# Planned attention: the inverse norms of queries and keys are spread by ScalarE instead of Pool

## The chip, the cores and the metric

The kernel runs on one core of a Trainium2 chip. The metric is the device time of one execution in microseconds (us); the number quoted for a kernel is the median of its runs. The engines are called as in the profile: PE multiplies matrices (PEld is its weight load, which overlaps), DVE is VectorE, ACT is ScalarE, POOL is GpSimd, SP issues most DMAs.

## What is computed

A causal trunk of two layers over 512 tokens of width 1024, float32 in and out. Layer 0 mixes with attention, layer 1 with a gated short convolution, and each is followed by a gated MLP of width 2816 with a width-3 convolution. Only the attention is touched:

```python
xn = rms_norm(h, norm_g)
proj = xn @ w_in                       # q, k, v of 16 heads of 64, and 8 gate logits
q_fox = rms_norm(q[:, :H_FOX], fox_q_gain)   # per head, over its 64 columns
k_fox = rms_norm(k[:, :H_FOX], fox_k_gain)
q_sb  = rms_norm(q[:, H_FOX:], sb_q_gain)
k_sb  = rms_norm(k[:, H_FOX:], sb_k_gain)
o_fox = forgetting_attention(q_fox, k_fox, v[:, :H_FOX], log_f)   # softmax with a decay
o_sb  = stick_breaking_attention(q_sb, k_sb, v[:, H_FOX:])        # sigmoids and a running product
return concat(o_fox, o_sb) @ w_out
```

`rms_norm` divides by the root of the mean square of the 64 columns of a head. The inverse norms are what the change handles.

## The kernel before, in words

Features lie on the 128 partitions and the 512 tokens along the free dimension. Each product of two float32 matrices is made of three PE passes: every operand is split into a rounded part `hi` (made by ACT) and a rest `lo` (made by DVE), and PE adds hi·hi, lo·hi and hi·lo into one PSUM bank (`mm3`, L435 to L440, for weights as the stationary operand; `mm3_rhs`, L620 to L623, for the values). Weights stream from HBM in tiles of about 0.5 MB (`raw`), which ACT copies to `whi` (L750) and DVE subtracts to `wlo` (L752).

The attention works on pairs of heads, eight pairs, in the order 4, 5, 6, 7 (stick-breaking), 0, 1, 2, 3 (forgetting). For each pair `queries_keys` (L885) does this:

- two dense projections into PSUM, 24 matmuls each, one for queries and one for keys; ACT evicts them (L908 or L916) and squares them (L913, L917);
- PE sums the squares over each head's 64 columns with a matrix of ones (L924), ACT copies the sums to SBUF (L927), and PE turns them so that tokens lie on the partitions (L928);
- DVE makes the inverse roots in a chain of small instructions, each of which needs the one before: L933, L945, three steps of Newton's method (L516 to L537), and L949. Their result is `qr`, 128 tokens by 16 numbers;
- **the spread, L960**: each of these numbers is written 64 times side by side into a tile `y` of 128 by 512, so that the four transposes of PE that follow (L967) put the inverse norm of each token under each of the head's 64 rows;
- DVE multiplies (L971), ACT makes `hi` (L973), DVE makes `lo` (L974). The scores of the pair (L1124) need these.

For the four forgetting pairs both queries and keys take this way; for the four stick-breaking pairs the queries alone, since the keys' norm goes into the scale of the sigmoid. So there are 4·2 + 4·1 = 12 spreads.

The order of the work in this part is not the order of the code. Every step is handed to a planner (`Plan`, L60 to L265) as an operation with an engine, a cost in us, what it reads and writes, and a rank. `order` (L191) lists the operations greedily: at each point it takes the engine that can begin something first, by its table of costs, and on that engine the operation of lowest rank among those that can begin within 0.03 us. A finished operation is seen by others after a fixed delay (`AFTER`: DVE 0.12, ACT 0.15, POOL 0.1). `choose` (L164) does so 60 times with the costs varied by up to 4%, replays each list four times with costs varied by 5%, and keeps the list that ends first on average. Dense projections are fillers: they have the highest ranks and go where nothing more urgent can begin on PE. The chosen list is issued in that order, and each engine then works through its own instructions strictly in order. An operation that the planner moves or re-prices can therefore move any other.

After the planned part (attention and its output projection) the rest of the kernel, MLP, convolution and second MLP, is written in program order and is the same in both kernels.

Of the kernel before, what the change touches and what calls it, by code (L numbers as in the profile page):

```python
# [23 lines left out]
AF = mybir.ActivationFunctionType  # L24
# [3 lines left out]
P = 128  # L28
S = 512
NB = S // P  # L30
# [4 lines left out]
HD = 64  # L35
# [233 lines left out]
def trunk(  # L269
# [7 lines left out]
    act, dve, pe, pool = nc.scalar, nc.vector, nc.tensor, nc.gpsimd  # L277
# [12 lines left out]
    def f32(ap):  # L290
        return ap.bitcast(F32)
# [125 lines left out]
    def weights(ahead=AHEAD):  # L417
        while len(ready) < min(len(wanted), at[0] + 1 + ahead):
            ready.append(load(len(ready)))
            split_all(len(ready) - 1)  # L420
        at[0] += 1
        return ready[at[0] - 1]
# [5 lines left out]
    def halves_of(x):  # L428
        return x.rearrange("p (two c) -> p two c", two=2)

    def sorted_(acc):

        return acc.rearrange("p (c two) -> p two c", two=2)
# [211 lines left out]
    plan = Plan()  # L645
# [48 lines left out]
    def DVE(us, fn, **k):  # L694
        return plan.op("DVE", us, fn, **k)

    def ACT(us, fn, **k):
        return plan.op("ACT", us, fn, **k)

    def PE(us, fn, **k):  # L700
        return plan.op("PE", us, fn, **k)

    def series(steps, r, w, rank, us=0.075):

        for i, fn in enumerate(steps):
            names[0] += 1
            key = ("series", names[0])
            DVE(us, fn, r=r, w=[key] if i < len(steps) - 1 else [key, *w], rank=rank)
            r = [key]
# [69 lines left out]
    def dense_part(bank_, w, k, part, seq):  # L779


        def fn():
            hi, lo = (turns(t) for t in x_of(k))
            w_hi, w_lo = w.get(k)
            if part:
                pe.matmul(bank_.tile, w_hi, lo, start=False, stop=k == ND - 1)
            else:
                pe.matmul(bank_.tile, w_hi, hi, start=k == 0, stop=False)
                pe.matmul(bank_.tile, w_lo, hi, start=False, stop=False)
        o = PE(0.216 if part else 0.432, fn, r=[*w.keys(k), (("hi", "lo")[part], k)], w=[bank_], rank=FILLER + seq)  # L790
        o.chunk = w.number
# [86 lines left out]
    def project_head(i, w, seq, ahead):  # L878
        b = acc_()
        for k in range(ND):  # L880
            dense(b, slice(None), w, k, lambda k=k: x_of(k), [("hi", k), ("lo", k)], k == 0, k == ND - 1, seq,
                  ahead=ahead if k == 0 else ())
        return b

    def queries_keys(p, ws, seq):  # L885

        fox, at0 = p < 4, CORE + 100 * PLACE[p]
        kept, sqs, got = {}, {}, {}
        banks = {}
        if seq is None:  # L890
            b = [acc_() for _ in range(2)]
            for k in range(ND):
                for part in range(2):
                    for i in range(2):
                        dense_part(b[i], ws[i], k, part, -FILLER + 20 + k + (ND * i if k >= 4 else 0))
            banks = dict(enumerate(b))
        for i in range(2):
            fixed = i == 1 and not fox
            if fixed:
                got[i] = half_["hi", i](), half_["lo", i]()  # L900
            else:
                kept[i] = kept_()
            b = banks[i] if i in banks else project_head(i, ws[i], seq + i, got[i] if fixed else [kept[i]])
            g = head_gains[:, (0 if fox else 2) + (1 - i):][:, 0:1]
            sq = sqs[i] = sq_()
            if fixed:
                hi, lo = got[i]
                ACT(0.57, lambda b=b, hi=hi, g=g: act.activation(halves_of(hi.tile), sorted_(b.tile), AF.Copy, scale=g),  # L908
                    r=[b, "head_gains"], w=[hi], rank=EVICT)
                DVE(0.66, lambda b=b, hi=hi, lo=lo, g=g: dve.scalar_tensor_tensor(  # L910
                    halves_of(lo.tile), sorted_(b.tile), g, halves_of(f32(hi.tile)), op0=ALU.mult, op1=ALU.subtract),
                    r=[b, hi, "head_gains"], w=[lo], rank=EVICT)
                ACT(0.49, lambda b=b, sq=sq: act.activation(halves_of(sq.tile), sorted_(b.tile), AF.Square), r=[b], w=[sq], rank=EVICT)  # L913
            else:
                n = kept[i]
                ACT(0.49, lambda b=b, n=n: act.activation(halves_of(n.tile), sorted_(b.tile), AF.Copy), r=[b], w=[n], rank=EVICT)  # L916
                ACT(0.52, lambda n=n, sq=sq: act.activation(sq.tile, n.tile, AF.Square), r=[n], w=[sq], rank=at0)  # L917

        t_sum, mid = turn_(), mid_()

        def sums():
            for i in range(2):
                for b in range(NB):
                    pe.matmul(t_sum.tile[32 * b:32 * (b + 1), 0:P], head_ones[:, i, :], sqs[i].tile[:, b * P:(b + 1) * P],  # L924
                              start=i == 0, stop=i == 1, tile_position=(0, 32 * b))
        PE(0.57, sums, r=[sqs[0], sqs[1]], w=[t_sum], rank=at0 + 2, mode="col", ahead=[mid])
        ACT(0.16, lambda: act.activation(mid.tile, t_sum.tile[:, 0:P], AF.Copy), r=[t_sum], w=[mid], rank=at0 + 2)  # L927
        PE(0.11, lambda: pe.transpose(t_sum.tile[:, P:2 * P], mid.tile, ident), r=[mid], w=[t_sum], rank=at0 + 2)  # L928
        made = {}

        def scaled():
            made["v"] = tiny.tile([P, NB, 4], F32, tag="qv", name=f"qv{p}")
            dve.tensor_tensor(  # L933
                made["v"], t_sum.tile[:, P:2 * P].rearrange("p (b c) -> p b c", b=NB)[:, :, 0:4], rx2[:, :, None].to_broadcast([P, NB, 4]), op=ALU.mult)
        DVE(0.09, scaled, r=[t_sum, "rx2"], w=[("v", p)], rank=at0 + 3)

        def v_():
            return made["v"].rearrange("p b i -> p (b i)")

        def r_():  # L940
            return made["r"].rearrange("p b i h -> p (b i h)")

        def add():
            made["r"] = tiny.tile([P, NB, 2, 2], F32, tag="qr", name=f"qr{p}")
            dve.tensor_scalar(v_(), v_(), EPS, None, op0=ALU.add)  # L945

        def by_norm():
            rf = made["r"].rearrange("p b i h -> p b (i h)")
            dve.tensor_tensor(rf, rf, norm.col[:, :, None].to_broadcast([P, NB, 4]), op=ALU.mult)  # L949
        series([add] + rsqrt(r_, v_, 16, f"qk{p}") + [by_norm], [("v", p)], [("r", p)], at0 + 3)  # L950
        if not fox:
            s = q_scale[p] = scales_()
            DVE(0.075, lambda: dve.tensor_copy(s.tile[:, 0], made["r"][:, :, 1, :]), r=[("r", p)], w=[(s, 0)], rank=at0 + 6)
            DVE(0.075, lambda: dve.tensor_scalar(s.tile[:, 1], made["r"][:, :, 1, :], -1.0, None, op0=ALU.mult),
                r=[("r", p)], w=[(s, 1)], rank=at0 + 6)
        for i in kept:
            t, wide, n = turn_(), y_(), kept[i]

            def spread(wide=wide, i=i):
                pool.tensor_copy(  # L960
                    wide.tile.rearrange("p (b h d) -> p b h d", b=NB, h=2),
                    made["r"][:, :, i, :][:, :, :, None].to_broadcast([P, NB, 2, HD]))
            plan.op("POOL", 1.0, spread, r=[("r", p)], w=[wide], rank=at0 + 4)

            def rows(t=t, wide=wide):
                for b in range(NB):
                    pe.transpose(t.tile[:, b * P:(b + 1) * P], wide.tile[:, b * P:(b + 1) * P], ident)  # L967
            hi, lo = got[i] = half_["hi", i](), half_["lo", i]()
            PE(0.436, rows, r=[wide], w=[t], rank=at0 + 4, ahead=[hi, lo])
            g = head_gains[:, (0 if fox else 2) + (1 - i):][:, 0:1]  # L970
            DVE(0.66, lambda t=t, n=n, g=g: dve.scalar_tensor_tensor(  # L971
                n.tile, n.tile, g, t.tile, op0=ALU.mult, op1=ALU.mult), r=[t, "head_gains"], w=[n], rank=at0 + 5)
            ACT(0.52, lambda n=n, hi=hi: act.activation(hi.tile, n.tile, AF.Copy), r=[n], w=[hi], rank=at0 + 5)  # L973
            DVE(0.6, lambda n=n, hi=hi, lo=lo: dve.tensor_tensor(lo.tile, n.tile, f32(hi.tile), op=ALU.subtract), r=[n, hi], w=[lo], rank=at0 + 5)  # L974
        halves[p] = got
# [384 lines left out]
    with tc.tile_pool(name="mlp0", bufs=1) as mp:  # L1360
# [3 lines left out]
        for o in range(ND):  # L1364
            acc = bank("ab"[o % 2])
            k = 0
            for nk in (8, 7, 7):
                w = weights()
# [7 lines left out]
    with tc.tile_pool(name="mix", bufs=1) as mp:  # L1376
# [23 lines left out]
        for o in range(ND):  # L1400
            w = weights()
# [7 lines left out]
    with tc.tile_pool(name="mlp1", bufs=1) as mp:  # L1409
# [13 lines left out]
        for c in range(2):  # L1423
# [23 lines left out]
            for k in range(k0):  # L1447
                if k % 2 == 0:
                    w = weights()
# [42 lines left out]
```

## Time and profile before

| what | value |
|---|---|
| median of 3 runs | 1116.42 us (1116.28, 1119.06, 1116.42) |
| the profiled execution's own time | 1118.01 us |
| its span, first to last instruction | 1116.2 us |
| granted PE clock | 1.000 |
| busy: PE / PEld / DVE / ACT / POOL | 1109.1 / 960.1 / 715.0 / 477.8 / 26.1 us |
| the 12 spreads on POOL | 10.7 us |

The profile shows one execution. A row of a timeline gives the start in us, the duration, engine, line, instruction, what it writes and reads, and in brackets how long its engine was idle just before and who ended that. Rows of the same kind that follow each other may be merged (x2). The duration of a matmul is a modelled one that overlaps its successor; the distance from start to start is what the matmul costs PE. A row of the windows view gives, for a stretch of time, each engine's busy time and its number of instructions.

### The profile page before, as it was taken

The page shows a single profiled execution, that of the slowest core. Times are in us where ns is not written, and L with a number is a line of the kernel's source. Part 1 is how long each engine was busy: PE and PEld are TensorE (multiplying, and loading weights), DVE is VectorE, ACT ScalarE, POOL GpSimd, SP SyncE. Part 2 cuts the span into 40 slices and gives each one's busy share as a digit, 9 for nine tenths or more (in the row PEclk, how much of TensorE's full clock was granted, in tenths as well). Part 3 has the DMA queues.
Part 4 walks back from the last instruction along what each step waited for, and adds up shares of the span by engine and source line. Part 5 has one row for each costly group of instructions (what it writes and reads, how often), then busy time and mean ns, then how long its engine had stood idle before and what let it go on. Part 6 is the DMA issues. An engine that isn't in the chain of part 4 may idle for free.

```text
span 1116.2 us, 14711 instructions
## 1 busy us (share of the span) xinstructions
PE 1109.1 (99%) x5781; PEld 960.1 (86%) x5781; DVE 715.0 (64%) x1117; ACT 477.8 (43%) x722; POOL 26.1 (2%) x92
## 2 busy tenths in 40 slices
PE   9999999999999999999999999999999999999998
PEld 8888788888888888888888888888888888888887
DVE  5898666767777777753334655556877777772322
ACT  6676655545444444432332323233444444442120
POOL 4000100000000000000000000000000000000000
PEclk9999999999999999999999999999999999999999
DMA  8434221223333333333333333333544333333441
GB/s 207 106 74 114 58 76 39 77 76 95 113 95 102 106 95 110 95 104 98 96 102 113 95 97 111 95 112 105 127 120 123 95 111 97 97 134 110 141 143 38
DMA packets 220933, 114.40 MB, mean 102 GB/s; under 512 B 39900, under 2 KB 213260, under 8 KB 220864
## 3 DMA queue, kind: packets, MB, share of 16 engines
q1 hardware_dynamic: 202416, 109.10, 33.5%
q10 hardware_dynamic: 18064, 4.20, 1.7%
q8 instruction: 45, 0.74, 0.3%
q0 software_dynamic: 384, 0.17, 0.1%
q14 instruction: 24, 0.20, 0.1%
HBM read 109.25 MB, written 4.19 MB: 102 GB/s over the span
## 4 chain that ended last, share of the span: by engine, by line
PE 91%; DVE 5%; DMA 1%; issue 1%; ACT 1%; SPq 1%; POOL 0%; DVEq 0%; POOLq 0%; ACTq 0%
PE psb L438 12%; PE psb L439 12%; PE psb L440 12%; PE psa L438 10%; PE psa L439 10%; PE psa L440 10%; PE acc L438 2%; PE acc L440 2%; PE acc L439 2%; PE psa L621 2%; PE psa L622 2%; PE psa L623 2%; PE psb L621 2%; PE psb L622 2%; PE psb L623 2%; PE score L1195 1%
## 5 line engine op out<-in xcount | busy, mean ns | idle before, releaser
L405 ACT ACTIVATE whi<-raw 128x1024 fp32r<-128x1024 f32 (+1 forms) x163 | 171.1, 1050 | 278.0 <-PE psb L439 97.0
L406 DVE TENSOR_TENSOR wlo<-raw,whi 128x1024 fp32r<-128x1024 f32 (+1 forms) x163 | 197.1, 1209 | 122.3 <-ACT whi L405 121.6
L438 PE MATMUL psb<-hs_hi,whi 128*128 128x512 f32 x480 | 182.7, 381 | 0.0
L439 PE MATMUL psb<-hs_lo,whi 128*128 128x512 f32 x480 | 181.9, 379 | 0.0
L440 PE MATMUL psb<-hs_hi,wlo 128*128 128x512 f32 x480 | 181.9, 379 | 0.0
L438 PE MATMUL psa<-hs_hi,whi 128*128 128x512 f32 x416 | 158.2, 380 | 0.0
L439 PE MATMUL psa<-hs_lo,whi 128*128 128x512 f32 x416 | 157.7, 379 | 0.0
L440 PE MATMUL psa<-hs_hi,wlo 128*128 128x512 f32 x416 | 157.7, 379 | 0.0
L553 DVE SCALAR_TENSOR_TENSOR u<-y,taps,u 128x510 f32<-128x510 f32 (+1 forms) x176 | 131.0, 747 | 5.2 <-ACT u L550 2.4
L440 PEld LDWEIGHTS psb<-hs_hi,wlo 128*128 128x128 f32 x480 | 90.7, 189 | 12.9
L439 PEld LDWEIGHTS psb<-hs_lo,whi 128*128 128x128 f32 x480 | 90.7, 189 | 12.6
L438 PEld LDWEIGHTS psb<-hs_hi,whi 128*128 128x128 f32 x480 | 90.7, 189 | 12.6
L440 PEld LDWEIGHTS psa<-hs_hi,wlo 128*128 128x128 f32 x416 | 78.6, 189 | 11.2
L439 PEld LDWEIGHTS psa<-hs_lo,whi 128*128 128x128 f32 x416 | 78.6, 189 | 11.0
L438 PEld LDWEIGHTS psa<-hs_hi,whi 128*128 128x128 f32 x416 | 78.6, 189 | 11.0
L545 ACT ACTIVATE a<-u 128x512 fp32r<-128x512 f32 x44 | 27.7, 630 | 118.0 <-DVE u L1347 118.0
L550 ACT ACTIVATE u<-y,taps 128x512 f32<-128x512 f32 x88 | 62.6, 714 | 12.0 <-DVE y L1335 12.0
L1335 DVE TENSOR_TENSOR y<-psb,nrow_n 128x512 f32<-128x512 f32 x44 | 30.4, 691 | 57.9 <-PE psb L440 57.9
L1346 ACT ACTIVATE u<-u 128x512 f32<-128x512 f32 x44 | 27.7, 629 | 85.9 <-DVE u L553 85.8
L752 DVE TENSOR_TENSOR wlo<-raw,whi 128x1024 fp32r<-128x1024 f32 (+2 forms) x41 | 43.8, 1075 | 19.0 <-ACT whi L750 18.8
L546 DVE TENSOR_TENSOR a<-u,a 128x512 fp32r<-128x512 f32 x44 | 30.4, 691 | 25.1 <-ACT a L545 25.1
L438 PE MATMUL acc<-hs_hi,whi 128*128 128x512 f32 x112 | 44.6, 398 | 0.0
(263 smaller groups left out, 1948.8 us busy)
## 6 DMA issues: line engine op xcount, KB each, us to landing
raw<-in_ffn_w_up SPq DMA_DIRECT2D x88, 512.0 KB, 3.8
raw<-in_ffn_w_down SPq DMA_DIRECT2D x30, 512.0 KB, 3.6
raw<-in_conv_w_in SPq DMA_DIRECT2D x24, 512.0 KB, 3.7
raw<-in_attn_w_in SPq DMA_DIRECT2D x20, 512.0 KB, 4.0
raw<-in_ffn_w_down SPq DMA_DIRECT2D x16, 448.0 KB, 3.3
raw<-in_attn_w_out SPq DMA_DIRECT2D x8, 512.0 KB, 3.4
raw<-in_conv_w_out SPq DMA_DIRECT2D x8, 512.0 KB, 3.5
big<-in_x SPq DMA_DIRECT2D x8, 256.0 KB, 4.2
```

The lines of the kernel that those rows point to most:

```text
L405: made = act.activation(hi[:, at_], raw[:, at_], AF.Copy)
L406: dve.tensor_tensor(lo[:, at_], raw[:, at_], f32(hi[:, at_]), op=ALU.subtract)
L438: pe.matmul(acc, w[0], hi, start=first, stop=False)
L439: pe.matmul(acc, w[0], lo, start=False, stop=False)
L440: pe.matmul(acc, w[1], hi, start=False, stop=last)
L546: dve.tensor_tensor(lo, src, f32(hi), op=ALU.subtract)
L550: act.activation(dst, src, AF.Copy, scale=tap(2))
L553: dve.scalar_tensor_tensor(dst[:, d:], src[:, 0:S - d], tap(j), dst[:, d:], op0=ALU.mult, op1=ALU.add)
L621: pe.matmul(acc, lhs[0], w[0], start=first, stop=False)
L622: pe.matmul(acc, lhs[0], w[1], start=False, stop=False)
L623: pe.matmul(acc, lhs[1], w[0], start=False, stop=last)
L752: DVE(dve_us(per * n), lambda: dve.tensor_tensor(self.lo.tile[:, at_], self.raw.tile[:, at_], f32(self.hi.tile[:, at_]), op=ALU.subtract), ...
```

## The change

The spread is issued on ACT, as an activation that copies, and no longer on POOL, and the planner is told so, with a cost of 0.49 us and no longer 1.0:

```diff
             def spread(wide=wide, i=i):
-                pool.tensor_copy(
+                act.activation(
                     wide.tile.rearrange("p (b h d) -> p b h d", b=NB, h=2),
-                    made["r"][:, :, i, :][:, :, :, None].to_broadcast([P, NB, 2, HD]))
-            plan.op("POOL", 1.0, spread, r=[("r", p)], w=[wide], rank=at0 + 4)
+                    made["r"][:, :, i, :][:, :, :, None].to_broadcast([P, NB, 2, HD]), AF.Copy)
+            plan.op("ACT", 0.49, spread, r=[("r", p)], w=[wide], rank=at0 + 4)
```

No other operation is added or removed: PE has the same matmuls on both sides, DVE and SP as many instructions as before, ACT has 12 more and POOL 12 fewer. But the planner makes a new list, and the order on every engine changes. Three places show it.

ACT, the first spread of all (pair 4; `y` is the spread tile, `qr` the inverse norms, `sq` squares, `qk_hi` rounded keys or queries, `whi` rounded weights, `v` values). Before:

```order
L917 ACTIVATE sq_511<-u_177_394 128x512
L908 ACTIVATE qk_hi_188_466<-acc_465,head_gains 128x512
L913 ACTIVATE sq_575<-acc_465 128x512
L750 ACTIVATE whi_585<-raw_479 128x1024
L1017 ACTIVATE v_556<-acc_555,ncol_n_445 128x256
L973 ACTIVATE qk_hi_211_634<-u_173_376 128x512
```

With the change:

```order
L917 ACTIVATE sq_502<-u_178_396 128x512
L908 ACTIVATE qk_hi_188_464<-acc_463,head_gains 128x512
L913 ACTIVATE sq_580<-acc_463 128x512
L960 ACTIVATE y_589<-qr_520 128x512
L750 ACTIVATE whi_598<-raw_472 128x1024
L1017 ACTIVATE v_562<-acc_561,ncol_n_436 128x256
L973 ACTIVATE qk_hi_205_601<-u_173_376 128x512
```

The spread stands between two activations that do not need it: the weights' copy and the eviction of values now stand behind an instruction that waits for DVE's chain.

PE, the transposes of pair 2, one of the forgetting pairs (`w` are attention weights that are turned, `acc` the banks of the values' projection). Before:

```order
L622 MATMUL acc_2474<-wlo_2520,hs_hi 128x256
L623 MATMUL acc_2474<-whi_2502,hs_lo 128x256
L1181 MATMUL turn_2546<-ident,w_2479 128x128 x3
L967 MATMUL turn_2550<-ident,y_2504 128x128 x4
L621 MATMUL acc_2474<-whi_2502,hs_hi 128x256
L622 MATMUL acc_2474<-wlo_2520,hs_hi 128x256
L623 MATMUL acc_2474<-whi_2502,hs_lo 128x256
L967 MATMUL turn_2562<-ident,y_2518 128x128 x4
```

With the change:

```order
L621 MATMUL acc_2579<-whi_2444,hs_hi 128x256
L622 MATMUL acc_2579<-wlo_2454,hs_hi 128x256
L623 MATMUL acc_2579<-whi_2444,hs_lo 128x256
L967 MATMUL turn_2587<-ident,y_2577 128x128 x4
L621 MATMUL acc_2579<-whi_2444,hs_hi 128x256
L622 MATMUL acc_2579<-wlo_2454,hs_hi 128x256
L623 MATMUL acc_2579<-whi_2444,hs_lo 128x256
L967 MATMUL turn_2600<-ident,y_2594 128x128 x4
```

The surroundings read alike, but the way back to the pair's L928 is shorter. Counted in the order, this many matmuls stand between L928 and the first L967 of a pair, for the pairs 4, 5, 6, 7, 0, 1, 2, 3: before 50, 116, 107, 119, 74, 89, 58, 39; now 36, 88, 61, 140, 42, 55, 39, 49. In the new order of pairs 0 and 2 these are all passes of the values' projection (L621 to L623).

ACT at the same pair 2 (`big` is an evicted attention output, `pt` turned weights). Before, with both spreads on POOL:

```order
L1186 ACTIVATE pt_2402<-turn_2546 128x3x128
L973 ACTIVATE qk_hi_531_2551<-u_459_2175 128x512
L1017 ACTIVATE v_2475<-acc_2474,ncol_n_445 128x256
L973 ACTIVATE qk_hi_534_2563<-u_476_2256 128x512
L1202 ACTIVATE big_2309<-score_2601 128x512
```

With the change:

```order
L1202 ACTIVATE big_2282<-score_2498 128x512
L1017 ACTIVATE v_2466<-acc_2465,ncol_n_436 128x256
L960 ACTIVATE y_2577<-qr_2522 128x512
L1017 ACTIVATE v_2466<-acc_2482,ncol_n_436 128x256
L960 ACTIVATE y_2594<-qr_2522 128x512
L973 ACTIVATE qk_hi_532_2588<-u_454_2157 128x512
```

Between the two spreads of the pair stands an eviction of values, and the eviction of the pair before (L1202, with L1203 on DVE behind it) now comes ahead of the spreads. Around L924 and L1195, which use PE in column groups, and L1124 and L1134, which use it in row groups, PE's passes between such and full matmuls are 53 in the new order and 50 in the old.

## The prediction

> **What bounds the kernel now.** I read the page first, then the busy times by stretch, then PE's own waits, then the rows around the transposes that need the spread.
>
> ```profile
> span 1116.2 us, 14711 instructions
> PE 1109.1 (99%) x5781; PEld 960.1 (86%) x5781; DVE 715.0 (64%) x1117; ACT 477.8 (43%) x722; POOL 26.1 (2%) x92
> ```
>
> PE is busy for 99% of the span. A change that leaves PE's matmuls as they are can only move the remaining waits. Busy times by stretch (start and end in us, length, then busy time and number of instructions of each engine):
>
> ```profile
> 22.00:236.00 214.00, 211.61 (x1576) 174.17 (x1575) 159.36 (x384) 133.06 (x284) 13.89 (x41) 1.00 0.31 80
> 236.00:1116.20 880.20, 876.72 (x4096) 768.11 (x4095) 545.31 (x712) 330.76 (x412) 0.00 (x0) 1.00 0.36 105
> ```
>
> All spreads lie in the first stretch, and POOL does nothing after it. There PE idles 214.00 − 211.61 = 2.4 us. That is a lower figure, since modelled ends of matmuls cover the first part of a wait. ACT has 81 us free and DVE 55. The second stretch runs the same instructions in both kernels. Who waits for the spread:
>
> ```profile
> L960 POOL COPY y<-qr x12: 610/799/1565, 35.8 to 208.5; 128x512 f32<-128x512 f32 x12
> PE turn L967 <- POOL y L960: 1.1, 2, 0.9
> PE turn L1181 <- DVE ga L1051: 0.4, 1, 0.4
> PE turn L967 <- DVE gains L1293: 0.3, 1, 0.3
> PE turn L1181 <- DVE w L1171: 0.3, 1, 0.3
> ```
>
> PE waited for POOL at two places only, of 12 spreads. At the other ten the copy was done in time. So the largest gain that the edit itself can have is what those two places cost, start to start:
>
> ```profile
> 127.43 0.28 PE L622 MATMUL acc<-wlo,hs_hi 128*128 128x256 f32 x1
> 127.55 0.28 PE L623 MATMUL acc<-whi,hs_lo 128*128 128x256 f32 x1
> 128.72 0.66 PE L967 MATMUL turn<-ident,y 128*128 128x128 f32 x4 [0.90 <-POOL y L960]
> 129.13 0.36 PE L621 MATMUL acc<-whi,hs_hi 128*128 128x256 f32 x1
> ...
> 207.85 0.38 PE L439 MATMUL acc<-o_lo,whi 128*128 128x512 f32 x1
> 208.07 0.38 PE L440 MATMUL acc<-big,wlo 128*128 128x512 f32 x1
> 208.63 0.66 PE L967 MATMUL turn<-ident,y 128*128 128x128 f32 x4 [0.18 <-POOL y L960]
> ```
>
> A 256-column pass costs PE 0.11 us (127.43 to 127.55), a 512-column pass 0.22 and four transposes 0.41. The first place thus lost 128.72 − 127.55 − 0.11 = 1.06 us, the second 208.63 − 208.07 − 0.22 = 0.34.
>
> **The change part by part.** *Removed*: 12 copies on POOL. The two waits go if the new copies come early enough: −1.4 us. Why were they late? The copy of the first place, and a tiny DVE instruction beside a copy and elsewhere:
>
> ```profile
> 126.97 1.23 DVE L752 TENSOR_TENSOR wlo<-raw,whi 128x1024 fp32r<-128x1024 f32 x1
> 127.10 2.78 POOL L960 COPY y<-qr 128x512 f32<-128x512 f32 x2 [1.57 <-DVE qr L949]
> ...
> 35.85 0.59 DVE L954 TENSOR_SCALAR qscale<-qr 128x8 f32<-128x8 f32 x1
> ...
> 100.77 0.16 DVE L954 TENSOR_SCALAR qscale<-qr 128x8 f32<-128x8 f32 x1
> ```
>
> A copy takes 0.61 us at best and 1.57 here, where it begins under a DVE subtraction of 1.23 us; and an 8-element DVE instruction that takes 0.16 us elsewhere takes 0.59 while a copy runs. The Trainium skill, "SBUF — State Buffer", section "Who interferes with whom", says that a DVE instruction with two SBUF inputs, or in a mode that uses two ports, and a GpSimd instruction that reads SBUF shut each other out for a whole instruction, and that ScalarE waits for nobody. Both rows agree. By that rule DVE gets time back too, which I price as a rival. My own sum gives it nothing, because DVE has 55 us free in the stretch and is named in PE's waits with 0.4, 0.3 and 0.3 us only.
>
> *Added*: 12 copies on ACT. The trace shows no activation that reads a repeated element, so I bound it by the nearest rows: 128 by 512 from SBUF, and twice that width.
>
> ```profile
> L917 ACT ACTIVATE sq<-u 128x512 f32<-128x512 f32 x12 | 7.7, 641 | 0.0
> L973 ACT ACTIVATE qk_hi<-u 128x512 fp32r<-128x512 f32 x12 | 7.6, 632 | 10.8 <-DVE u L971 10.7
> L1017 ACT ACTIVATE v<-acc,ncol_n 128x256 f32<-128x256 f32 x16 | 7.6, 475 | 2.4 <-PE acc L623 2.1 <-DVE gate L1024 0.3
> L750 ACT ACTIVATE whi<-raw 128x1024 fp32r<-128x1024 f32 x25 | 26.7, 1068 | 3.8 <-issue 3.2 <-PE acc L623 0.6
> ```
>
> I take 0.63 us (ends 0.60 and 1.07): 12 · 0.63 = 7.6 us more ACT, hidden in its 81 free us. What counts is the instant at which `y` is ready against the instant at which PE gets to L967. The planner now prices the copy at 0.49 + 0.15 us and not at 1.0 + 0.1, so it puts L967 about 0.46 us sooner after the inverse roots, and the count of matmuls between L928 and L967 falls for six of eight pairs. The roots take as long as before. One whole chain without strangers in it:
>
> ```profile
> 144.09 0.17 DVE L933 TENSOR_TENSOR qv<-turn,rx 128x16 f32<-128x16 f32 x1
> ...
> 144.50 0.17 DVE L516 TENSOR_SCALAR rh_qk<-qv 128x16 f32<-128x16 f32 x1
> ...
> 146.88 0.17 DVE L949 TENSOR_TENSOR qr<-qr,ncol_n 128x16 f32<-128x16 f32 x1
> ```
>
> From L933 it is 146.88 + 0.17 − 144.09 = 2.96 us, and from L516 2.55. I take the three places with the shortest cover.
>
> *Pair 0* has 42 passes of 256 columns between: 42 · 0.11 = 4.6 us, plus 0.1 for L928. On DVE L1203 stands inside the chain, ahead of L516, and waits for ACT's L1202, which waits for L1195, PE's work just ahead of L928. Before, the same sequence:
>
> ```profile
> 88.02 0.65 PE L924 MATMUL turn<-sq,head_ones 128*32 128x128 f32 x16
> 88.13 0.60 ACT L1202 ACTIVATE big<-score 128x512 fp32r<-128x512 f32 x1 [2.84 <-PE score L1195]
> 88.77 0.69 DVE L1203 TENSOR_TENSOR o_lo<-score,big 128x512 fp32r<-128x512 f32 x1 [0.99 <-ACT big L1202]
> ```
>
> L1203 ends 88.77 + 0.69 − 88.02 = 1.44 us after PE left L1195; 2.55 more make 4.0; ACT's copy 0.63 and two handovers of 0.05 (L1202 to L1203 above took 0.04) make 4.73. PE arrives at 4.7, and 0.41 later wants the second copy, which ACT has 0.63 after the first: together 0.2 us lost.
>
> *Pair 2* has 39 passes: 4.3 + 0.1 = 4.4, so PE waits 0.3. Its second copy stands behind an eviction of values (0.48 us); PE wants it 0.41 + 0.33 us after the first, while ACT needs 0.48 + 0.63, less what back-to-back activations overlap: 0.3 more, 0.6 in all.
>
> *Pair 4*, the first:
>
> ```profile
> 32.99 0.28 PE L621 MATMUL acc<-whi,hs_hi 128*128 128x264 f32 x1
> ...
> 37.35 0.28 PE L623 MATMUL acc<-whi,hs_lo 128*128 128x264 f32 x1
> 37.96 0.63 PE L967 MATMUL turn<-ident,y 128*128 128x128 f32 x4 [0.33 <-DVE gains L1293]
> ...
> 34.90 0.75 DVE L910 SCALAR_TENSOR_TENSOR qk_lo<-acc,head_gains,qk_hi 128x512 fp32r<-128x512 f32 x1
> 35.57 0.17 DVE L949 TENSOR_TENSOR qr<-qr,ncol_n 128x16 f32<-128x16 f32 x1
> ```
>
> Here PE lost 37.96 − 37.35 − 0.11 = 0.5 us to another reader of the same PSUM ring. Now L967 comes after 18 passes of the values' projection, at 32.99 + 18 · 0.11 = 35.0. L910 now stands behind the chain, so L949 ends near 35.57 + 0.17 − 0.67 = 35.1 and the copy at 35.75: 0.8 us lost, 0.3 more than before. Queued behind the copy on ACT, which waits there for the chain, are the weights' copy L750 and an eviction; PE needs those weights only after some hundred more passes, so nobody waits.
>
> *Pairs 6, 1 and 3* have 61, 55 and 49 rows between, with strangers in DVE's chain. I give each 0.2 us (from 0 to 0.6): 0.6.
>
> *Passes between full and grouped matmuls* rise from 50 to 53. The first full matmul after a grouped one costs more:
>
> ```profile
> 29.54 0.48 PE L438 MATMUL acc<-hs_hi,whi 128*128 128x512 f32 x1
> 29.86 0.38 PE L439 MATMUL acc<-hs_lo,whi 128*128 128x512 f32 x1
> 30.07 0.38 PE L440 MATMUL acc<-hs_hi,wlo 128*128 128x512 f32 x1
> ```
>
> 0.32 us against 0.21, so 0.1 on the way in. What the way out costs these rows do not separate; I let it be 0 to 0.1. Three passes more are 0.3 to 0.6 us: +0.4.
>
> *The rest of the new list* (score activations, weights, other transposes) I take at zero: other waits of the same kind and number, with ends of −1 us, about the three named waits on DVE, and +3 us, 0.4 us at each of the eight pairs.
>
> Sum: −1.4 + 0.2 + 0.6 + 0.3 + 0.6 + 0.4 = +0.7 us. The span would be 1116.9. The profiled execution took 1118.0, 1.8 more than its span; the median of the runs is 1116.42, near the span, so I add there: **1117.1 us**.
>
> **The rivals.** *A, DVE is freed.* With no copy on POOL, no DVE instruction is shut out, and the waits on DVE go with those on POOL: 1.1 + 0.4 + 0.3 + 0.3 = 2.1 us, at most the 2.4 us that PE idles in the stretch. Time 1114.0. For it speak the 0.59 against 0.16 us; against it that only these small waits name DVE, and that the planner's new list spends any slack by placing L967 sooner.
>
> *B, ACT's queue becomes the wait (the slower side).* ACT works in order. Where the chain on DVE is late, the spread holds ACT, and the score activations, evictions and weights behind it come late, then DVE's products, then PE's transposes. The planner's costs have no slack left: by its own numbers the copy is ready just when PE arrives. If each of eight pairs loses 0.6 us this way beyond my sum, it is 4.8 us: 1121. It decides once L949 comes more than about 0.5 us later, against PE, than the planner took it. For it: DVE is 89% busy between 60 and 100 us.
>
> ```profile
> 60.00:100.00 40.00, 39.68 (x306) 31.93 (x306) 35.61 (x90) 25.06 (x53) 1.70 (x12) 1.00 0.37 80
> ```
>
> Against it: dense passes are there as fillers, and before the change PE idled just 0.3 us in this very stretch.
>
> *C, a dearer copy.* The broadcast copy on ACT could cost more than its like, up to 1.07 us; then each wait above grows by 0.4 us, in the range below.
>
> **How the numbers follow.** My forecast has 0.64, A 0.15, B 0.15, C (about 1118.5) 0.06. The range goes from A's time, 1114.0, to just short of B's, 1120.6, and so leaves out B's far half and what A could gain beyond the idle time shown. A measurement of this kernel can tell about 0.3%, 3.35 us, from no change: below 1113.1 or above 1119.8. Faster than that would need nearly all of PE's idle time in the stretch and more: 0.04. Slower is most of B: 0.13. Within: 0.83.
>
> **What would show it.** In the profile after: no waits of PE for POOL; L960 on ACT at 0.60 to 0.65 us; L967 waiting for ACT at pairs 4 and 2 with 0.3 to 0.8 us each; L954 at 0.16 us throughout; PE's idle time between 22 and 236 us within 1 us of 2.4. I am wrong if the stretch from 236 us on changes its length, if PE's idle time there falls under 1 us (A), or if it rises over 5 us with ACT waiting at L960 and PE waiting for what stands behind it (B).

## The result, and the profile after

| | median of runs | profiled execution | its span |
|---|---|---|---|
| before | 1116.34 us (21 runs, 1116.00 to 1119.06) | 1118.01 us | 1116.2 us |
| changed | 1114.50 us (21 runs, 1114.16 to 1116.32) | 1114.38 us | 1112.6 us |

The changed kernel is faster by 1.84 us: ratio 0.9982, 95% interval 0.9976 to 0.9988. The forecast was 0.7 us slower. The change lies inside the 0.3% that I called no change, but the sign was wrong: the interval leaves out the forecast's 0.7 us slower, and no change as well.

The two spans differ by 3.6 us, twice what the medians do, so the first thing to settle is which part of that belongs to the change. I divide each execution at two instants that both kernels have: the one L1272 matmul (a transpose of the gains of the norms, ahead of all spreads) and the first matmul of the MLP (the first that writes a `psa` bank). The windows view of before (start and end, length, busy time and instructions of each engine):

```profile
16.75:258.69 241.94, 239.55 (x1706) 198.63 (x1705) 180.29 (x416) 151.14 (x313) 13.89 (x41) 1.00 0.32 83
258.69:1116.20 857.51, 854.02 (x3991) 748.26 (x3989) 527.15 (x687) 317.90 (x394) 0.00 (x0) 1.00 0.36 105
```

The same two instants in the changed kernel:

```profile
15.34:255.06 239.72, 238.98 (x1706) 198.33 (x1706) 176.89 (x416) 156.83 (x325) 3.49 (x29) 1.00 0.33 84
255.06:1112.60 857.54, 854.02 (x3991) 748.26 (x3989) 526.93 (x687) 317.78 (x394) 0.00 (x0) 1.00 0.35 105
```

And in a second profiled execution of before (the run e0 below):

```profile
15.71:257.33 241.62, 239.49 (x1705) 198.64 (x1705) 180.29 (x416) 151.03 (x313) 13.90 (x41) 1.00 0.33 84
257.33:1114.90 857.57, 854.03 (x3991) 748.26 (x3989) 527.09 (x687) 317.85 (x394) 0.00 (x0) 1.00 0.36 105
```

What follows the planned part takes 857.5 us in all three, with the same 3991 matmuls. The start varies from execution to execution (16.75 and 15.71 us with one kernel). The planned part is 241.6 to 241.9 us before and 239.7 after, 1.9 to 2.2 us shorter, about the difference of the medians. There PE idles 241.62 − 239.49 = 2.1 us before and 239.72 − 238.98 = 0.74 after. From here on "the planned part" is this stretch, and before is taken from its second execution.

Who is waited for in the changed kernel: the spread's own view, L954's, and PE's waits.

```profile
L960 ACT ACTIVATE y<-qr x12: 617/629/664, 33.5 to 206.2; 128x512 f32<-128x512 f32 x12
...
L954 DVE TENSOR_SCALAR qscale<-qr x4: 163/164/166, 33.6 to 94.6; 128x8 f32<-128x8 f32 x4
...
PE turn L967 <- ACT y L960: 0.4, 1, 0.4
PE turn L1181 <- DVE w L1171: 0.2, 1, 0.2
```

Read against before: POOL is gone from the list, the copy takes 0.63 us (min, median, max in ns), the 8-element L954 is always short. But PE waits at one of the transposes only, where I had expected it at several, and two of the three waits for DVE of the first execution are gone too.

### The profile page after: what moved, and what is told of

It is laid out like the page before. It is cut to its first block, busy times and chain, and to the rows that moved or that the text cites. A ratio compares the mean times of both kernels' runs of the same rounds, so it can differ in the third digit from the quotient of the medians.

```text
span 1112.6 us, 14692 instructions
## 1 busy us (share of the span) xinstructions
PE 1107.1 (100%) x5781; PEld 958.4 (86%) x5781; DVE 711.4 (64%) x1117; ACT 483.6 (43%) x734; POOL 15.7 (1%) x80
## 4 chain that ended last, share of the span: by engine, by line
PE 98%; DVE 1%; DMA 0%; SPq 0%; issue 0%; ACT 0%; DVEq 0%
PE psb L438 12%; PE psb L440 12%; PE psb L439 12%; PE psa L438 10%; PE psa L439 10%; PE psa L440 10%; PE acc L438 3%; PE acc L439 3%; PE acc L440 3%; PE turn L1181 2%; PE score L1124 2%; PE psa L623 2%; PE psa L621 2%; PE psa L622 2%; PE score L1195 2%; PE psb L623 2%
```

## The experiments

Two theories stood at the start. *Engine*: a copy on ACT is ready sooner or lets DVE run, so PE's waits go. *Order*: the planner, told another engine and another price, makes another list, and the list is the better one, whatever engine does the copy. The two parts of the change can be had apart, since the engine that issues the copy and the engine that the planner is told are separate arguments. Each ratio below is to before, timed in the same session (medians of 1116.5 to 1116.6 us).

**Before, once more** (e0): the reference for all that follows.

> The kernel before, once more, to get a second profile of it. The first profile was of an execution of 1118.0 us, 1.7 above the median, and it differs from the one after by 3.6 us of span where the medians differ by 1.8. Theory 'chance at the start': of those 3.6 us, 1.4 were lost in the first 16 us, where PE ran its 512-column passes at 0.43 us and not at 0.22 until 10 us; a typical execution leaves that pace earlier, and this profile's span is about 1114.5, with L1272 near 15.4 us and not 16.75. Theory 'belongs to the list': the span is 1116 again and L1272 near 16.7. Timed against the kernel before it is 1.000 under both.

Measured 1116.38 us, ratio 0.9998 (0.9989 to 1.0007). The profile's span is 1114.9 us and L1272 stands at 15.71: near what chance at the start had said, 0.3 to 0.4 us later, and far from the other theory.

**The engine alone** (e1): the copy is issued on ACT, the planner is told what it was told before; PE's order is that of before.

```diff
-            plan.op("ACT", 0.49, spread, r=[("r", p)], w=[wide], rank=at0 + 4)
+            plan.op("POOL", 1.0, spread, r=[("r", p)], w=[wide], rank=at0 + 4)
```

> The copy runs on ACT, but the planner is still told POOL and 1.0 us: every other engine has the order of before, word for word, and ACT has the 12 copies put into it where the list has them. Theory 'engine' (the copy comes sooner, and POOL and DVE no longer shut each other out): 1114.5 to 1115, the whole gain or the 1.4 us of the two waits for POOL, with L967 waiting for nobody at 127.6 and 208 us. Theory 'list' (the gain is the new order of the other operations): 1116.3, no gain, or up to 1 us worse where the copies hold up ACT.

Measured 1116.8 us, ratio 1.0004 (0.9995 to 1.0013): by the medians the engine alone gains nothing. The place where the old list lost 1.06 us to POOL shows why. ACT, and then PE, in the timeline of e1:

```profile
126.15 0.59 ACT L1186 ACTIVATE pt<-turn 128x512 f32<-128x512 f32 x1
126.63 0.63 ACT L960 ACTIVATE y<-qr 128x512 f32<-128x512 f32 x1
...
129.06 0.65 ACT L973 ACTIVATE qk_hi<-u 128x512 fp32r<-128x512 f32 x1
129.58 0.49 ACT L1017 ACTIVATE v<-acc,ncol_n 128x256 f32<-128x256 f32 x1
...
129.36 0.28 PE L623 MATMUL acc<-whi,hs_lo 128*128 128x256 f32 x1
130.12 0.48 PE L438 MATMUL acc<-hs_hi,whi 128*128 128x512 f32 x1 [0.48 <-ACT v L1017]
```

The copies went into a stretch in which ACT works without a gap, and pushed back what stands behind them; the eviction L1017 came late and PE waited for the bank: 130.12 − 129.36 − 0.11 = 0.65 us. That is near rival B, ACT's queue becoming the wait, at one place; but the copies delay by the time they take, and not because they wait for DVE's chain, as B had it. DVE got its time back here, 178.10 us busy in e1's planned part against 180.29, and the median shows nothing of the 2.1 us that rival A had priced.

```profile
15.64:256.69 241.05, 239.56 (x1705) 198.67 (x1705) 178.10 (x416) 156.95 (x325) 3.31 (x29) 1.00 0.33 84
```

In this one execution, the fastest of e1's, the planned part is 0.6 us shorter than in that of e0 (241.05 for 241.62). The interval of the ratio just allows as much, so a small share of the copy's own engine is not excluded.

**The list alone** (e2): the copy stays on POOL, the planner is told ACT at 0.49 us; PE's order is that of the changed kernel.

```diff
-            plan.op("POOL", 1.0, spread, r=[("r", p)], w=[wide], rank=at0 + 4)
+            plan.op("ACT", 0.49, spread, r=[("r", p)], w=[wide], rank=at0 + 4)
```

> The copy stays on POOL, but the planner is told ACT and 0.49 us: every other engine has the order of after, word for word, ACT without the copies. Theory 'engine': no gain, 1116.3 or more, since L967 now comes sooner than POOL's copies of 0.6 to 1.6 us (about 0.5 us lost at each of pairs 4, 0, 2, some 1118). Theory 'list': the gain stays, 1114.5 to 1115.

Measured 1114.72 us, ratio 0.9982 (0.9973 to 0.9990): the whole gain without the copy on ACT. PE's waits are those of the changed kernel, with POOL in ACT's place, and e2's planned part takes 240.01 us, 1.6 us less than before and 0.3 more than in the changed kernel:

```profile
PE turn L967 <- POOL y L960: 0.4, 1, 0.4
PE turn L1181 <- DVE w L1171: 0.2, 1, 0.2
...
15.46:255.47 240.01, 239.21 (x1705) 198.14 (x1705) 178.28 (x416) 150.73 (x313) 11.54 (x41) 1.00 0.33 84
```

DVE is busy for 178.28 us here, as in e1 (178.10), and the medians are 2.1 us apart. So the time that DVE gets back does not make the gain: that is rival A refuted.

**POOL at a lower price** (e3): before, with 0.54 in place of 1.0, so that the planner puts the transposes sooner.

> The copy stays on POOL and the planner is told POOL, but with 0.54 us, so that with POOL's 0.1 us of delay it is as dear as on ACT (0.64). The order differs from that of before in few places. Theory 'engine': 1116.3 to 1117.5, no gain, with longer waits for POOL. Theory 'list, through the price': the planner puts L967 sooner and everything behind it gains: 1114.5 to 1115.5.

Measured 1117.82 us, ratio 1.0012 (1.0003 to 1.0021). PE's waits at the transposes after the copy's two slow places, with the copies on POOL:

```profile
125.48 0.28 PE L623 MATMUL acc<-whi,hs_lo 128*128 128x256 f32 x1
126.99 0.66 PE L967 MATMUL turn<-ident,y 128*128 128x128 f32 x4 [1.23 <-POOL y L960]
...
206.33 0.38 PE L440 MATMUL acc<-big,wlo 128*128 128x512 f32 x1
207.54 1.21 PE L967 MATMUL turn<-ident,y 128*128 128x128 f32 x8 [0.83 <-POOL y L960]
...
125.37 2.78 POOL L960 COPY y<-qr 128x512 f32<-128x512 f32 x2 [1.57 <-DVE qr L949]
```

1.40 and 0.99 us, where before lost 1.06 and 0.35: a price under the truth is paid at the next wait. The time lies 0.3 us above the range of the engine theory, whose mechanism it shows, and against "list, through the price": a lower price told for POOL does not make the better list.

So on this draw of the list it is order (e1, e2). But is the new list better for a reason (theory P, the planner makes better lists when it is told ACT) or is it a lucky one (theory L)? `choose` varies the costs by random numbers; other numbers give other lists of the same kind.

**Other draws** (s1, s2, s5 of before; s3, s4, s6 of the changed kernel): in `choose`, with 10000, 20000 and 30000 for the second, third and fourth draw,

```diff
-            draw.seed(seed)
+            draw.seed(seed + 10000)
```

> The kernel before (copy on POOL, cost 1.0), but the planner varies its costs with other random numbers, so that it keeps another list of the same kind. Nothing else is changed. If lists of this planner differ by luck (theory L), this one lies anywhere between about 1114 and 1119 us, and the spread among lists with the copy on POOL is as large as the 1.8 us between the two kernels compared. If telling the planner of ACT and 0.49 us is what makes better lists (theory P), this one is at 1116.4, within 0.5.

> As the first, with a third set of random numbers. Theory L: 1114 to 1119 us, and not the same as the first. Theory P: 1116.4, within 0.5.

> The changed kernel (copy on ACT, cost 0.49) with other random numbers in the planner. Theory L: anywhere between about 1114 and 1119 us, as likely above 1116.4 as below. Theory P: 1114.6, within 0.5.

> As the one before, with a third set of random numbers. Theory L: 1114 to 1119 us, and not the same as the other. Theory P: 1114.6, within 0.5.

> The kernel before (copy on POOL, cost 1.0) with a fourth set of random numbers in the planner. Its lists so far: 1116.5, 1114.9, 1115.6 us. Theory P (telling the planner of ACT and 0.49 us makes better lists): above 1114.6, the slowest so far of the changed kernel. Theory L (luck alone): as likely below as above 1114.7, the middle of the six lists.

> The changed kernel with a fourth set of random numbers. Its lists so far: 1114.6, 1112.1, 1113.0 us. Theory P: below 1114.9, the fastest so far with the copy on POOL. Theory L: as likely above as below 1114.7.

| list and copy | first draw | second | third | fourth |
|---|---|---|---|---|
| made for POOL at 1.0, copy on POOL | 1116.4 | 1114.9 | 1115.6 | 1115.8 |
| made for ACT at 0.49, copy on ACT | 1114.5 | 1112.1 | 1113.0 | 1113.3 |

As worded, both theories missed. P had 1116.4 and 1114.6 within 0.5, and all four lists of the second and third draw lie lower; L had 1114 to 1119, and two of them lie below (1112.1 and 1113.0). The fourth draw came as the milder P of its expectations said. Luck moves a list by up to 1.5 us in the first row and 2.4 in the second. Still every list made for ACT beats every list made for POOL; of six new lists the three fastest would fall so by chance 1 time in 20. The second draw of the changed kernel is the fastest version of all, 1112.06 us, ratio 0.9960 (0.9947 to 0.9974). In its planned part PE idles 237.24 − 237.11 = 0.13 us, and no wait is left for its view to list:

```profile
15.48:252.72 237.24, 237.11 (x1706) 198.51 (x1705) 176.84 (x416) 156.49 (x325) 3.28 (x29) 1.00 0.33 85
```

**List and engine crossed on the second draw** (p2: list made for ACT, copy on POOL; r1: list made for POOL, copy on ACT), edits as in e2 and e1, with the second draw's 10000.

> The list of the changed kernel's second draw (1112.1 us with the copy on ACT), told to the planner as ACT at 0.49, with the copy issued on POOL. If the order alone makes the time, also on this list: 1112.1, within 0.5. If ACT's copy is needed for it (the copy on POOL takes 0.6 to 1.6 us and shuts DVE out, and this list places the transposes tightly): 1113 to 1115, with PE waiting for POOL at the transposes.

> The second draw's list made for POOL at 1.0 us (1114.9 us with the copy on POOL, PE's waits for POOL 1.5 us in sum), with the copy issued on ACT. If the list makes the time (order): 1114.9, within 0.7, as on the first draw, where ACT in the old list gave 1116.8 for 1116.6. If the copy's engine makes it: 1114.9 less the waits of 1.5 us, 1113.4 or less, toward the 1112.1 of the list made for ACT.

p2 took 1112.82 us, ratio 0.9965 (0.9953 to 0.9977), and r1 1115.70, ratio 0.9991 (0.9982 to 1.0000). The list decides again: 1112.1 and 1112.8 with the one, 1114.9 and 1115.7 with the other. But both lie outside what order had allowed, on the slow side, p2 by 0.2 us and r1 by 0.1: on this draw a copy on the engine that the list was not made for costs 0.8 us by the medians (0.6 by the ratios), where on the first it cost 0.2 (0.4 or less). The engine theory had r1 at 1113.4 or less, and p2 with waits of PE for POOL, of which there are none. The list of p2 bears copies as slow as those of before, because PE comes later there: these two end at 125.46 and 126.68, and PE begins its transposes at 127.04 and 129.49.

```profile
123.90 2.78 POOL L960 COPY y<-qr 128x512 f32<-128x512 f32 x2 [1.53 <-DVE qr L949]
```

**The price alone.** If lists made for ACT are better, is it the engine told (theory E) or that POOL's price of 1.0 is too low where DVE shuts the copy out (theory V)? p1: the changed kernel with ACT at 1.0; q3: with ACT at 0.64, what it takes; q4: the second draw with ACT at 1.0. q1 and q2: POOL at 1.6 on the first and second draw. r2: the list of e3 (POOL at 0.54), with the copy on ACT. The edit is the number in `plan.op`; for q1:

```diff
-            plan.op("POOL", 1.0, spread, r=[("r", p)], w=[wide], rank=at0 + 4)
+            plan.op("POOL", 1.6, spread, r=[("r", p)], w=[wide], rank=at0 + 4)
```

> The changed kernel, but the planner is told 1.0 us for the copy on ACT and not 0.49: the engine changes, the price stays. The first random numbers. If the better lists come from the lower price, which lets the planner put the transposes sooner behind the roots, this one is near the lists of before: 1115 to 1117 us. If they come from the copy's being placed in ACT's queue at all, it is near the lists of the changed kernel: 1112 to 1114.6.

> The kernel before, with the copy on POOL told at 1.6 us and not 1.0: about what it takes where DVE shuts it out. If the price was the fault (theory V), the planner leaves room, PE's two waits for POOL (1.06 and 0.35 us) go, and the time falls by 1.4 us or more from 1116.5, to 1115.1 or less. If the engine told is what counts (theory E), the list is one like the others of POOL: 1114.9 to 1116.6, and no better on average than at 1.0.

> The same on the second draw of random numbers, where POOL at 1.0 us took 1114.9 us with waits for POOL of 0.73, 0.39 and 0.40 us. Theory V: 1.5 us less, 1113.4, within 0.7. Theory E: 1114.9 to 1116.6.

> The changed kernel (first draw) with the copy on ACT told at 0.64 us, what it takes, and not 0.49. The first pair's transposes, which waited 0.57 us for ACT, then get 0.15 us more room. A list like the others told as ACT's: 1112.1 to 1114.6; if an honest price helps, 0.2 to 0.6 us under 1114.6; if the price is of no account, anywhere in the group.

> The changed kernel, second draw, with the copy on ACT told at 1.0 us. On the first draw the price of 1.0 gave 1113.9 against 1114.6 at 0.49. If a price above the truth buys room for the transposes at no cost: 1112.1 or less. If it delays the pairs' scores: 1112.5 to 1114.

> The list made for POOL at 0.54 us (first draw; 1117.8 us with the copy on POOL), with the copy issued on ACT, where it takes 0.63 us. PE's waits at the transposes (3.7 us in sum there, against 2.2 in the kernel before) should fall to about 1. If the list made for POOL is worse in itself: 1116 or more, since what ACT does late then delays others. If an honest cost is all that matters: 1114.6, like the lists told as ACT's.

| run | median us | ratio to before, 95% |
|---|---|---|
| p1, ACT told at 1.0 | 1113.93 | 0.9979 (0.9971 to 0.9988) |
| q3, ACT told at 0.64 | 1114.41 | 0.9982 (0.9973 to 0.9991) |
| q4, ACT told at 1.0, second draw | 1114.71 | 0.9986 (0.9977 to 0.9995) |
| q1, POOL told at 1.6 | 1115.67 | 0.9994 (0.9985 to 1.0003) |
| q2, POOL told at 1.6, second draw | 1114.59 | 0.9984 (0.9975 to 0.9992) |
| r2, list of POOL at 0.54, copy on ACT | 1116.61 | 1.0000 (0.9991 to 1.0009) |

q1 lies inside theory E's range, q2 between the two. Nobody waits for POOL any more in either, as theory V said, but neither is faster than its list at 1.0 by more than the noise: q1's interval contains no change, and q2's 0.9984 stands against 0.9986 for the second draw at 1.0. PE's waits in q1 tell where the time went:

```profile
PE acc L621 <- DVE qk_lo L910: 0.5, 1, 0.5
PE score L1124 <- DVE qk_lo L974: 0.2, 1, 0.2
PE turn L1181 <- ACT v L1017: 0.2, 1, 0.2
```

The room for the copy was given back as waits elsewhere. p1, where the engine told changes and the price of 1.0 stays, lies in the range that its expectation gave to the copy's place in ACT's queue; a lower price is not needed. With ACT the price hardly shows on the first draw (1114.5, 1114.4 and 1113.9 at 0.49, 0.64 and 1.0); the room that q3 should have given the first pair's transposes did not come either, they lost 0.58 us, as at 0.49. On the second draw 1.0 cost 2.6 us against 0.49 (1114.7 against 1112.1), more than either case of its expectation allowed; I take the second draw at 0.49 for a lucky one as well, which is not shown. In r2 PE's waits at L967 fell from e3's 3.7 us to 1.5, not quite the 1 expected, and the time by 1.2 us, to that of before: a list made for POOL is not saved by a copy that keeps its price.

In sum, seven lists made for ACT, with the copy there, took 1112.1 to 1114.7 us (mean 1113.7), and seven made for POOL, with the copy there, 1114.6 to 1117.8 (mean 1115.8). The groups touch, and they are not fourteen independent draws, since some share a draw and differ in the price. Shown, on the two draws where list and engine were crossed, is that the order makes the gain: the list made for ACT is faster by 1.7 to 3.6 us with the copy on either engine. That lists made for ACT are better in general rests on four draws.

Where the better lists gain can be read from the profiles, of one execution each. The planned parts of the four draws made for POOL take 241.6, 240.1, 240.6 and 241.1 us, with PE idle for 2.1, 1.1, 1.7 and 1.9 of it; of the four made for ACT 239.7, 237.2, 238.3 and 238.5, with 0.7, 0.1, 0.4 and 0.6. So about half of the difference, or more, is PE waiting less. Part of the rest can be PE's passes between full and grouped matmuls: 42, 42, 42 and 44 in the first four, and 48, 38, 40 and 40 in the second. They fell in three draws, the fastest list has the fewest, and they rose in the one under test; so they are no common cause.

What in the planner's greedy rule makes the better lists is not settled. That POOL's price is too low was not shown to be a part of it. One reason that I can argue and did not isolate is that only a list made for ACT leaves room for the copy in ACT's queue; it explains e1, r1 and r2, but not why e2 and p2 are good with the copy on POOL.

## Why the prediction was wrong, point by point

*The wait for POOL goes, −1.4 us:* right. In the second execution of before the two places lost 1.06 and 0.35 us, in the changed kernel neither is there. But the reason was not the engine, as e2 shows: with the copy on POOL they are gone as well, and no DVE instruction runs beside the copies there. The copies of pairs 0 and 3 in e2, two each, took 1.16 and 1.17 us together, where pair 0's had taken 2.78:

```profile
131.63 1.16 POOL L960 COPY y<-qr 128x512 f32<-128x512 f32 x2 [13.20 <-DVE qr L949]
...
206.19 1.17 POOL L960 COPY y<-qr 128x512 f32<-128x512 f32 x2 [21.81 <-DVE qr L949]
```

The slow copy did not vanish: in e2 it is the first of pair 1, 1.67 us, and PE lost 0.07 us behind it.

*The copy's own cost, 0.63 us:* right, 0.617 to 0.664. Rival C is out.

*The places with a short cover, +1.7 us for pairs 0, 2, 4, 6, 1 and 3:* **this is the step that failed first.** It took the roots' chain to be as long as before while the cover of matmuls shrinks, and put the instant of `y` against PE's with rough costs. Leaving out the two places above, PE's waits at all L967, start to start, sum to 0.83 us before and 0.67 after: −0.2, and not +1.7.

Pair 4 went as worked out, a little cheaper. PE, DVE and ACT after:

```profile
33.50 0.28 PE L623 MATMUL acc<-whi,hs_lo 128*128 128x264 f32 x1
34.19 0.66 PE L967 MATMUL turn<-ident,y 128*128 128x128 f32 x4 [0.41 <-ACT y L960]
...
33.29 0.17 DVE L949 TENSOR_TENSOR qr<-qr,ncol_n 128x16 f32<-128x16 f32 x1
...
33.50 0.63 ACT L960 ACTIVATE y<-qr 128x512 f32<-128x512 f32 x1 [0.54 <-DVE qr L949]
```

34.19 − 33.50 − 0.11 = 0.58 us lost, against 0.8 forecast and 0.5 before: +0.1 instead of +0.3. Pair 0 was the closest call:

```profile
127.33 0.33 PE L928 MATMUL turn<-ident,mid 128*128 128x128 f32 x1
127.42 0.36 PE L621 MATMUL acc<-whi,hs_hi 128*128 128x256 f32 x1
127.61 0.28 PE L622 MATMUL acc<-wlo,hs_hi 128*128 128x256 f32 x1
...
132.07 0.28 PE L623 MATMUL acc<-whi,hs_lo 128*128 128x256 f32 x1
132.19 1.08 PE L967 MATMUL turn<-ident,y 128*128 128x128 f32 x8
...
131.05 0.18 DVE L949 TENSOR_TENSOR qr<-qr,ncol_n 128x16 f32<-128x16 f32 x1
...
131.42 1.14 ACT L960 ACTIVATE y<-qr 128x512 f32<-128x512 f32 x2
```

From PE's last L1195 on I had `y` at 4.73 us and PE at 4.7. Counted from L928, `y` is ready after 131.42 + 0.62 − 127.33 = 4.71 (the roots' chain was 0.1 us shorter than I had it, and the copy then stood behind an eviction for 0.2), but PE needs 132.19 − 127.33 = 4.86 us for its 42 passes: the first pass after a transpose costs 0.19 and the others 0.1115, not 0.11. The second copy ends 0.52 us after the first, not 0.63, because two activations in a row overlap by 0.1; I had allowed for that at pair 2 and not here. So nothing is lost: the first copy is there 0.15 us before PE, and the second 0.06 (132.62 − 132.56), about what the handover to PE takes (0.06 at pair 4, 34.19 − 33.50 − 0.63). At pair 2 the forecast 0.6 us came to 0.15:

```profile
183.13 0.28 PE L623 MATMUL acc<-whi,hs_lo 128*128 128x256 f32 x1
183.34 0.66 PE L967 MATMUL turn<-ident,y 128*128 128x128 f32 x4
...
184.22 0.66 PE L967 MATMUL turn<-ident,y 128*128 128x128 f32 x4
...
182.66 0.63 ACT L960 ACTIVATE y<-qr 128x512 f32<-128x512 f32 x1 [1.75 <-DVE qr L949]
...
183.55 0.62 ACT L960 ACTIVATE y<-qr 128x512 f32<-128x512 f32 x1
```

At the first copy 183.34 − 183.13 − 0.11 = 0.1 us: counted from L928 at 178.73, `y` is ready at 4.56 and not 4.73, and PE would come at 4.51 and not 4.4. At the second 0.05 and not 0.3: PE wants it 0.83 us after the first, since a pass behind a transpose costs 0.19 here too, and gets it after 0.88. At pairs 6, 1 and 3, for which I had put down 0.2 us each without working them out, PE lost nothing. A shorter cover was bought by a shorter chain, which the count of matmuls does not show. Pair 6 before, from L928 to the roots' last step:

```profile
70.78 0.27 PE L928 MATMUL turn<-ident,mid 128*128 128x128 f32 x1
...
86.90 0.17 DVE L949 TENSOR_TENSOR qr<-qr,ncol_n 128x16 f32<-128x16 f32 x1
```

16.1 us start to start; and in the changed kernel:

```profile
73.73 0.27 PE L928 MATMUL turn<-ident,mid 128*128 128x128 f32 x1
...
82.46 0.16 DVE L949 TENSOR_TENSOR qr<-qr,ncol_n 128x16 f32<-128x16 f32 x1
82.66 0.63 ACT L960 ACTIVATE y<-qr 128x512 f32<-128x512 f32 x1 [0.67 <-DVE qr L949]
```

8.7 us, with 61 matmuls between L928 and L967 for 107 (77 for 123 with the 16 of L924 that stand just ahead of L967 in both). "The roots take as long as before" was false for the pairs whose chain had strangers in it.

*The rest of the new list, at zero with ends of −1 and +3:* the second failure in size, and at the very end of its range. PE's waits for the transposes of attention weights (L1181) fell from 1.7 to 1.1 us, and the remaining ones by 0.4: −1.0.

*Passes between full and grouped matmuls, +0.4:* the right kind, with a wrong count. The 53 and 50 given for the two orders also count passes between column and row groups; between full and grouped matmuls there are 48 and 42, six more and not three. Taking for each kind of neighbouring matmuls (by group and width) its usual distance start to start, the new list's matmuls alone sum to 0.6 us more.

These measured terms, −1.4 − 0.2 − 1.0 + 0.6, are −2.0, against −1.9 for the planned part itself. How the last two divide depends on how finely the kinds are told apart: with the lines kept apart too the matmuls' own share is only 0.1 to 0.3 us, and the waits fell by correspondingly less. The sign of my +0.7 hung on the +1.7 under either: with −0.2 in its place the sum is −1.2.

*The rivals.* A's time came nearly true (1114.0 against 1114.5), by luck, since its mechanism did not. The Trainium skill, "SBUF — State Buffer", section "Who interferes with whom", says that the lock holds between DVE and GpSimd and that ScalarE waits for nobody; the rows agree (POOL's first copy of pair 0 takes 1.56 us, ACT's at most 0.71 in any list), but on PE's path the lock's price is in what the planner does not know: it reckons with 1.0. Something like B was seen in e1 at one place. (B's time should have been 1121.9: 4.8 us beyond my 1117.1; nothing hung on it.) None of my cases had the planner simply making better lists.

*What would show it.* No wait for POOL, L960 at 0.62 to 0.66 us, L954 always short and the wait at pair 4 came as said; the wait of 0.3 to 0.8 us at pair 2 did not. PE's idle time fell to 0.74 us, under the 1 us that I had given to A: I read it as A's mark, and it was not. And the stretch from 236 us on was a bad test: a kernel that reaches its MLP sooner has a shorter stretch (876.6 for 880.2 us) though the same work follows. Nor does that stretch run the same instructions in both kernels, as I had said: the planned part reaches to 258.69 us in the first execution of before. Bounds at the same instruction would have been right.

## What to carry to other kernels

Where a planner sets the order, a new price or engine for one small operation is a new list, and the gain or loss of the operation itself may be the smaller part: tell the list from the engine by issuing on one and planning for the other, before explaining anything. A list is one draw; lists of one kind spread here by up to 2.4 us, more than the change moved the time, so compare several draws of each kind. A cover counted in matmuls says nothing until the chain that it covers has been worked out in the same list.

## What the runs showed of the hardware

The time to L1272 was 16.75 and 15.71 us in two executions of one kernel, though the granted clock is shown as 1.00 from the start. Passes of 512 columns at the start, in the first execution of before:

```profile
7.13 0.63 PE L789 MATMUL acc<-hs_hi,wlo 128*128 128x512 f32 x1
7.55 0.63 PE L786 MATMUL acc<-hs_lo,whi 128*128 128x512 f32 x1
...
9.55 0.77 PE L788 MATMUL acc<-hs_hi,whi 128*128 128x512 f32 x1
10.11 0.42 PE L789 MATMUL acc<-hs_hi,wlo 128*128 128x512 f32 x1
10.37 0.38 PE L786 MATMUL acc<-hs_lo,whi 128*128 128x512 f32 x1
```

And in the profiled execution of the changed kernel, 1.6 us later:

```profile
8.75 0.38 PE L789 MATMUL acc<-hs_hi,wlo 128*128 128x512 f32 x1
8.96 0.38 PE L786 MATMUL acc<-hs_lo,whi 128*128 128x512 f32 x1
```

0.42 us start to start against 0.21. In the first execution of before the slow pace holds until about 10 us (0.56 and then 0.26). The Trainium skill, "TensorE: Matmul & The Clock Gate", Part 1, says that the array starts at half rate and goes to full rate after a window of some 3.4 us of work, whose phase is free, so that the instant differs from run to run; these rows agree with the two paces, and with an instant that moves. It belongs to the execution and not to the kernel; the planned part, which begins after it, is shorter by 1.9 us without it.
